# The first two up-projection tiles in token halves, ahead of the second half's norm

## The chip, the cores and the metric

The kernel runs on one core of a Trainium2 chip. The metric is the device time of one execution in microseconds, given as the median of several executions of the same program. The engines in what follows are PE (TensorE, matmuls), PEld (its weight loads), DVE (VectorE), ACT (ScalarE), POOL (GpSimd) and SP (the queue that issues DMAs).

## What is computed

One layer of a decoder trunk: attention and a state-space model side by side, an output projection, then a gated MLP. There are 256 tokens, 2048 model columns and 5632 columns in the MLP. The change is at the seam between the output projection and the MLP's up projection. Cut to what is computed there:

```python
mix = merged @ w_out                              # 256 x 2048
x = x + (1.0 + gt_m) * rmsnorm(mix, g_post_mix)
h = rmsnorm(x, g_pre_ffn) * (1.0 + sc_f) + sh_f   # 256 x 2048
up = causal_depthwise_conv(h @ w_up, conv_w, conv_b)   # 2048 -> 2 x 5632
val, gate = up[..., :D_FF], up[..., D_FF:]
ff = (gelu(gate) * val) @ w_down
x = x + (1.0 + gt_f) * rmsnorm(ff, g_post_ffn)
```

## The kernel before

The output projection accumulates `mix` in eight banks of PSUM, `acc[tt * 4 + n]`: two halves `tt` of 128 tokens by four quarters `n` of 512 columns. The last three of its 16 chunks are held back and then run bank by bank (`proj_held`, nine matmuls of 128x512 each), so that a bank is done while the next ones still run.

For each token half and quarter the seam then does: a square and sum of the bank on ACT (`sq`), a product with the gain on DVE (`gain`), and once all four sums of a half are there, its rstd (`rstd_start`, `rstd_end`; the last step, a power, runs on POOL). With it `x_add` makes the new x on DVE and `x_turn` transposes it on PE, four transposes of 128x128 to a quarter. `x_scale` takes them out of PSUM on DVE. `x_split` writes them as two numbers, a high part (a cast on ACT) and a low part (a subtraction on DVE or POOL, by its last argument: "ag" is ACT and POOL, "av" is ACT and DVE), into the four tiles `h2`, each of which holds four chunks of 128 model columns, and in each chunk the high parts of 256 tokens and then the low parts.

The up projection has 88 tiles, `up_mm(f, vg, parts)`, for 44 values of `f` and value or gate. Each reads 1 MB of weights, which `hl_up` loads and splits into high and low parts in two pieces (`h_wup`, `l_wup`, 128x1024 each, in a pool of five buffers of each kind). A tile is 16 chunks of two matmuls: the high weights against high and low tokens (512 columns) and the low weights against the high tokens (256 columns), both in a 32-bit type rounded for the matmul.

The scale by the second norm's rstd is put off: it is a factor of each token, made beside the first tiles (eight squares of x on ACT, two small matmuls with a diagonal, `ps_rn`), and `up_tile` applies it after the matmul. Between the tiles PE also computes the MLP's shift vector from weight granules (`ps_ada`, 32 matmuls to a pair of granules, and two column sums by `sel`).

What sets the order: PE's order follows the code through this seam, and so do DVE, ACT and POOL, since `in_order` adds a dependency from each of their instructions to the one before. Past the seam a scheduler places the instructions of all engines but SP, and so lets the shift matmuls slip between those of the tiles. SP issues its DMAs in the order of the code. The raw loads share six buffers of 1 MB (`raw`, and the two `prods`).

## Time and profile before

| | us |
|---|---|
| median of the three timed runs (1186.97 to 1190.68) | 1189.53 |
| the profiled execution | 1187.82 |
| its span in the profile | 1186.0 |
| PE busy in the span | 1128.9 |
| DVE busy | 874.6 |
| ACT busy | 547.2 |

The profile is of one execution, and its rows count from the start of the span. A row of the timeline gives the start, the time for which it lasts, the engine, the line, what is written and read, and what the engine waited for. Starts of one engine's rows may overlap: an instruction is in flight while the next begins, so the distance between starts says what one costs in a row of them. Plain f32 matmuls and transposes are recorded with their passes, so a plain f32 matmul has two records.

### The profile page before, as it was taken

The numbers are of one execution on the slowest core, as the hardware profiler recorded it, in microseconds if no ns is written. First come the engines' busy times: TensorE is split into PE (matmuls) and PEld (weight loads), VectorE is DVE, ScalarE is ACT, GpSimd is POOL, SyncE is SP. The second block draws the span as 40 slices with busy tenths as digits, with TensorE's granted clock in tenths as the row PEclk, the third lists the DMA queues.
The fourth block names the chain that finished last, engine by engine and source line by source line (L and its number), as shares of the span: only waits on it lengthen the run. The fifth ranks groups of instructions, "written<-read, shape, count | busy, mean of one in ns | idle before, by whom it ended". The sixth has DMA issues, their size and how long they took to land.

```text
span 1186.0 us, 18905 instructions
## 1 busy us (share of the span) xinstructions
PE 1128.9 (95%) x7542; PEld 945.5 (80%) x7542; DVE 874.6 (74%) x1386; ACT 547.2 (46%) x911; POOL 109.2 (9%) x107
## 2 busy tenths in 40 slices
PE   6999996988999799999999999999999999999996
PEld 4788875767787588888888888888888788888885
DVE  6687645775699778668999998986676766767555
ACT  3222131362534364446666556555555544444443
POOL 7404111004200320000000000000000000000002
PEclk8999999898999899999999999999999999999998
DMA  9899989388799668886787777775555787777712
GB/s 383 309 371 340 363 279 342 121 353 320 261 343 391 241 253 337 326 297 249 255 313 284 283 284 290 279 283 188 203 178 189 259 296 280 264 298 280 264 69 72
DMA packets 50234, 325.88 MB, mean 275 GB/s; under 512 B 6609, under 2 KB 8833, under 8 KB 13537
## 3 DMA queue, kind: packets, MB, share of 16 engines
q1 hardware_dynamic: 47152, 316.87, 71.7%
q0 software_dynamic: 2848, 7.75, 2.0%
q8 instruction: 59, 0.97, 0.3%
q14 instruction: 31, 0.25, 0.1%
q10 hardware_dynamic: 144, 0.05, 0.0%
HBM read 317.27 MB, written 7.37 MB: 274 GB/s over the span
## 4 chain that ended last, share of the span: by engine, by line
PE 77%; DVE 10%; issue 7%; DMA 3%; ACT 2%; POOL 1%; SPq 0%; DVEq 0%; ACTq 0%; POOLq 0%
PE ps_u L1235 28%; PE dn L562 15%; PE ps_u L1237 14%; PE accA L395 8%; PE ps_ada L155 3%; DVE l_wout L72 2%; PE ps_g L1033 2%; DVE ada L142 2%; PE accB L603 1%; DMA U<-ud 1%; PE mix L553 1%; DMA wglu<-in_w_glu_dram 1%; DVE scn L72 1%; DMA ud<-uT 1%; PE ps_y L809 1%
## 5 line engine op out<-in xcount | busy, mean ns | idle before, releaser
L543 ACT CAST h_wup<-wup 128x1024 fp32r<-128x1024 f32 x170 | 178.8, 1052 | 196.6 <-PE ps_u L1235 181.2
L544 DVE TENSOR_TENSOR l_wup<-wup,h_wup 128x1024 fp32r<-128x1024 f32 x170 | 207.9, 1223 | 83.3 <-ACT h_wup L543 79.8
L1235 PE MATMUL ps_u<-h2A,h_wup 128*128 128x512 f32 x704 | 251.5, 398 | 0.0
L1235 PE MATMUL ps_u<-h2B,h_wup 128*128 128x512 f32 x704 | 249.1, 394 | 0.0
L1237 PE MATMUL ps_u<-h2A,l_wup 128*128 128x256 f32 x704 | 196.4, 279 | 0.0
L1237 PE MATMUL ps_u<-h2B,l_wup 128*128 128x256 f32 x704 | 195.8, 278 | 0.0
L1235 PEld LDWEIGHTS ps_u<-h2A,h_wup 128*128 128x128 f32 x704 | 132.8, 189 | 31.3 <-issue 1.0
L1235 PEld LDWEIGHTS ps_u<-h2B,h_wup 128*128 128x128 f32 x704 | 132.0, 188 | 30.9 <-issue 0.4
L544 DVE TENSOR_TENSOR l_wdn<-wdn,h_wdn 128x1024 fp32r<-128x1024 f32 x88 | 107.6, 1224 | 65.7 <-ACT h_wdn L543 65.6
L1237 PEld LDWEIGHTS ps_u<-h2A,l_wup 128*128 128x128 f32 x704 | 133.2, 189 | 0.6 <-issue 0.4
L1237 PEld LDWEIGHTS ps_u<-h2B,l_wup 128*128 128x128 f32 x704 | 132.3, 188 | 0.4 <-issue 0.4
L543 ACT CAST h_wdn<-wdn 128x1024 fp32r<-128x1024 f32 x88 | 92.6, 1053 | 78.7 <-PE dn L562 70.4
L395 PE MATMUL accA<-hT,win 128*128 128x256 f32 x448 | 108.1, 387 | 0.0
L562 PE MATMUL dn<-h_wdn,fl 128*128 128x512 f32 x336 | 104.6, 396 | 1.4 <-DVE fl L544 1.4
L562 PE MATMUL dn<-l_wdn,fh 128*128 128x512 f32 x336 | 105.7, 395 | 0.0
L562 PE MATMUL dn<-h_wdn,fh 128*128 128x512 f32 x336 | 105.5, 396 | 0.0
L395 PEld LDWEIGHTS accA<-hT,win 128*128 128x128 f32 x448 | 82.0, 191 | 14.8 <-issue 5.1
L142 DVE CUSTOM_DVE_ANT_0 ada<-ada,cbc 128x2048 f32<-128x2048 f32 x38 | 87.8, 2319 | 0.2 <-DMA ada<-in_w_ada_dram 0.2
L562 PEld LDWEIGHTS dn<-h_wdn,fl 128*128 128x128 f32 x336 | 63.0, 188 | 17.0 <-DVE fl L544 1.9
L562 PEld LDWEIGHTS dn<-l_wdn,fh 128*128 128x128 f32 x336 | 63.1, 188 | 15.3
L562 PEld LDWEIGHTS dn<-h_wdn,fh 128*128 128x128 f32 x336 | 63.1, 188 | 15.2
L1377 DVE CUSTOM_DVE_ANT_0 wupt<-wupt,shbc 128x2048 f32<-128x2048 f32 x22 | 50.2, 2284 | 0.5 <-DMA wupt<-in_w_up_t_dram 0.5
(356 smaller groups left out, 1517.5 us busy)
## 6 DMA issues: line engine op xcount, KB each, us to landing
wup<-in_w_up_dram SPq DMA_DIRECT2D x88, 1024.0 KB, 5.0
ada<-in_w_ada_dram SPq DMA_DIRECT2D x64, 1024.0 KB, 6.8
wdn<-in_w_down_dram SPq DMA_DIRECT2D x44, 1024.0 KB, 4.9
wupt<-in_w_up_t_dram SPq DMA_DIRECT2D x22, 1024.0 KB, 6.3
scm<-in_w_ada_dram SPq DMA_DIRECT2D x16, 1024.0 KB, 9.0
shm<-in_w_ada_dram SPq DMA_DIRECT2D x16, 1024.0 KB, 6.1
wout<-in_w_out_dram SPq DMA_DIRECT2D x16, 1024.0 KB, 6.2
win<-in_w_in_a_dram SPq DMA_DIRECT2D x16, 896.0 KB, 7.4
```

The source lines that it names most:

```text
L72: self.last = self.no_earlier(getattr(self.e, name)(*args, **kw))
L142: return nc.vector.tensor_tensor_reduce(t, t, cbc, 1.0, 0.0, ALU.mult, ALU.add, accum_out=dst)
L155: PE.matmul(ps[32 * j:32 * j + 32, v * P:(v + 1) * P], lhsT=csil[:, kc:kc + 1].to_broadcast([P, 32]), rhs=t[:, kc * P:(kc + 1) * P], start ...
L395: PE.matmul(accA[ct // 2][:, (ct % 2) * S:(ct % 2 + 1) * S], lhsT=winA[k][:, ct * P:(ct + 1) * P], rhs=hk, start=(k == 0 and ct % 2 == 0), ...
L543: (A.copy if e[0] == "a" else V.tensor_copy)(hi, src)
L544: (V if e[1] == "v" else G).tensor_sub(lo, src, hi.bitcast(F32))
L553: PE.matmul(acc[tt * 4 + n], lhsT=a_[:, tk], rhs=b_[:, n2 * 512:(n2 + 1) * 512], start=False, stop=(kk == nk - 1 and last))
L562: PE.matmul(acc[tt * 4 + half * 2 + n2], lhsT=a_[:, tk], rhs=b_[:, n2 * 512:(n2 + 1) * 512], start=(kk == 0 and first), stop=(kk == nk - 1 ...
L1033: PE.matmul(psg[ct][:, :S], lhsT=wg_[ct // 2][:, (ct % 2 * 8 + k) * P:(ct % 2 * 8 + k + 1) * P], rhs=zf[:, k], start=(k == 0), stop=(k == 7))
L1235: PE.matmul(ps, lhsT=wh[:, ks], rhs=h2[kk // 4][:, kk % 4].rearrange("p a b -> p (a b)"), start=(kk == 0), stop=(kk == KD - 1), skip_group ...
L1237: PE.matmul(ps[:, :S], lhsT=wl[:, ks], rhs=h2_of(kk)[0], start=False, stop=(kk == KD - 1), skip_group_check=True)
L1377: V.tensor_tensor_reduce(t, t, shbc[0], 1.0, 0.0, ALU.mult, ALU.add, accum_out=rlate[:, vg, f:f + 1])
```

## The change

A new helper, `up_half(ps, parts, tt)`, does an up tile for one half of the tokens: 16 chunks of a matmul with 2 x 128 columns (high and low tokens of the half) and one with 128 columns. Tiles (0, 0) and (0, 1), which were two calls of `up_mm`, become four calls of it, each with 32 matmuls, and two of the four stand among the steps of the second half's norm. The weights of tile (0, 1) are loaded and split earlier in the code. The last two held banks of the second token half now stand behind the four `x_add` of the first half, and its last `x_split` has its low part on DVE instead of POOL. Tile (1, 0) is computed where (0, 1) was, and the weights of (1, 1) are asked for there.

```diff
+    def up_half(ps, parts, tt):
+
+        tk = slice(tt * P, (tt + 1) * P)
+        pv2 = ps.rearrange("p (a b) -> p a b", a=2)
+        for half in range(2):
+            wh, wl = parts[half]
+            for k in range(8):
+                kk, ks = half * 8 + k, slice(k * P, (k + 1) * P)
+                PE.matmul(pv2[:, :, tk], lhsT=wh[:, ks], rhs=h2[kk // 4][:, kk % 4, :, tk], start=(tt == 0 and kk == 0),
+                          stop=(kk == KD - 1), skip_group_check=True)
+                PE.matmul(ps[:, tk], lhsT=wl[:, ks], rhs=h2_of(kk)[0][:, tk], start=False, stop=(kk == KD - 1),
+                          skip_group_check=True)
...
-    for n in range(3):
-        proj_held(acc, held, 1, n)
+    proj_held(acc, held, 1, 0)
+    proj_held(acc, held, 1, 1)
     x_add(0, 0)
     sq(1, 0)
     gain(1, 0)
     x_add(0, 1)
     sq(1, 1)
     gain(1, 1)
-    proj_held(acc, held, 1, 3)
     x_scale(0, 0)
     x_split(0, 0, "ag")
     x_add(0, 2)
     x_scale(0, 1)
-    sq(1, 2)
     x_split(0, 1, "ag")
     x_add(0, 3)
+    proj_held(acc, held, 1, 2)
+    x_scale(0, 2)
+    x_split(0, 2, "ag")
+    sq(1, 2)
+    x_scale(0, 3)
+    x_split(0, 3, "av")
     rstd_start(24, nrm[:, 2, 1:2])
     gain(1, 2)
+    proj_held(acc, held, 1, 3)
+
+    ups.append(hl_up(0, 1, "ag"))
+    early = [bank(0, "ps_u")]
+    up_half(early[0], ups[0], 0)
     sq(1, 3)
-    x_scale(0, 2)
     rstd_end(24)
     gain(1, 3)
-    x_scale(0, 3)
-    x_split(0, 2, "ag")
-    x_split(0, 3, "ag")
     x_add(1, 0)
     x_add(1, 1)
+    early.append(bank(1, "ps_u"))
     x_scale(1, 0)
     x_split(1, 0, "ag")
     x_add(1, 2)
     x_scale(1, 1)
     x_split(1, 1, "ag")
+    up_half(early[1], ups[1], 0)
     x_add(1, 3)
     x_scale(1, 2)
     x_scale(1, 3)
     x_split(1, 2, "av")
     x_split(1, 3, "av")
-    early = [up_mm(0, 0, ups.pop(0))]
-    ups.extend((hl_up(0, 1, "ag"), hl_up(1, 0)))
+    up_half(early[0], ups.pop(0), 1)
+    up_half(early[1], ups.pop(0), 1)
+    ups.append(hl_up(1, 0))
...
-    early.append(up_mm(0, 1, ups.pop(0)))
+    ups.append(hl_up(1, 1))
+    early.append(up_mm(1, 0, ups.pop(0)))
...
-        if 2 < n_ < 2 * KF:
+        if 3 < n_ < 2 * KF:
             ups.append(hl_up(n_ // 2, n_ % 2))
-        ps = up_mm(f, vg, ups.pop(0)) if f else early[vg]
+        ps = early.pop(0) if early else up_mm(f, vg, ups.pop(0))
```

Three places in the order of the instructions follow. The names are the program's: `mix_2643` is the sixth held bank, `mix_2704` and `mix_2705` the seventh and the eighth, `ps_x` the transposes, `x_3184` and `x_3186` the x of the first and of the second token half, `prod_3204` and `prod_3205` their products, `stat` the sums and the rstd.

PE before, from the end of the eighth held bank to the first up tile:

```order
L553 MATMUL mix_2705<-l_wout,mh_2980 128x512
L553 MATMUL mix_2705<-h_wout,ml_2754 128x512
L1217 MATMUL ps_x_3316<-c_71,x_3184 128x128 x4
L1217 MATMUL ps_x_3327<-c_71,x_3184 128x128 x4
L1217 MATMUL ps_x_3347<-c_71,x_3186 128x128 x4
L1217 MATMUL ps_x_3353<-c_71,x_3186 128x128 x4
L1217 MATMUL ps_x_3362<-c_71,x_3186 128x128 x4
L1217 MATMUL ps_x_3371<-c_71,x_3186 128x128 x4
L1235 MATMUL ps_u<-h2A_3200,h_wup 128x512
```

PE now, from the end of the sixth held bank to the start of the seventh:

```order
L553 MATMUL mix_2643<-l_wout,mh_2980 128x512
L553 MATMUL mix_2643<-h_wout,ml_2754 128x512
L1217 MATMUL ps_x_3277<-c_71,x_3184 128x128 x4
L1217 MATMUL ps_x_3286<-c_71,x_3184 128x128 x4
L1217 MATMUL ps_x_3298<-c_71,x_3184 128x128 x4
L1217 MATMUL ps_x_3307<-c_71,x_3184 128x128 x4
L553 MATMUL mix_2704<-h_wout,mh_2935 128x512
```

PE now, from the end of tile (0, 0)'s first half to the start of tile (0, 1)'s first half:

```order
L1237 MATMUL ps_u<-h2B_3203,h_wup 128x2x128
L1239 MATMUL ps_u<-h2B_3203,l_wup 128x128
L1217 MATMUL ps_x_3390<-c_71,x_3186 128x128 x4
L1217 MATMUL ps_x_3396<-c_71,x_3186 128x128 x4
L1217 MATMUL ps_x_3406<-c_71,x_3186 128x128 x4
L1237 MATMUL ps_u<-h2A_3200,h_wup 128x2x128
L1239 MATMUL ps_u<-h2A_3200,l_wup 128x128
```

All 16 transposes of the first half now stand ahead of the seventh and the eighth bank, where two quarters stood ahead of the eighth and two behind it; and a half tile stands between the first half's transposes and the second's.

ACT before, from the first cast of a token quarter to the first weight cast:

```order
L72 CAST h2A_3200<-prod_3204 128x4x128
L72 ACTIVATE junk,stat<-mix_2704 128x512
L72 CAST h2A_3201<-prod_3204 128x4x128
L72 ACTIVATE junk,stat<-mix_2705 128x512
L72 CAST h2B_3202<-prod_3204 128x4x128
L72 CAST h2B_3203<-prod_3204 128x4x128
L72 CAST h2A_3200<-prod_3205 128x4x128
L72 CAST h2A_3201<-prod_3205 128x4x128
L72 CAST h2B_3202<-prod_3205 128x4x128
L72 CAST h2B_3203<-prod_3205 128x4x128
L72 CAST h_wup<-wup_3415 128x1024 x2
```

ACT now, in the same place:

```order
L72 CAST h2A_3200<-prod_3204 128x4x128
L72 CAST h2A_3201<-prod_3204 128x4x128
L72 CAST h2B_3202<-prod_3204 128x4x128
L72 ACTIVATE junk,stat<-mix_2704 128x512
L72 CAST h2B_3203<-prod_3204 128x4x128
L72 CAST h_wup<-wup_3341 128x1024 x2
L72 ACTIVATE junk,stat<-mix_2705 128x512
L72 CAST h2A_3200<-prod_3205 128x4x128
```

The weight casts of tile (0, 1) have moved from behind all token casts to a place ahead of the eighth bank's square.

POOL, the difference from before (-) to now (+), from the low parts of the first token half on:

```order
 L72 TENSOR_TENSOR h2A_3200<-prod_3204,h2A_3200 128x4x128
 L72 TENSOR_TENSOR h2A_3201<-prod_3204,h2A_3201 128x4x128
+L72 TENSOR_TENSOR h2B_3202<-prod_3204,h2B_3202 128x4x128
+L72 TENSOR_TENSOR l_wup<-wup_3341,h_wup 128x1024 x2
 L72 TENSOR_TENSOR stat<-stat,neg_half 128x1
-L72 TENSOR_TENSOR h2B_3202<-prod_3204,h2B_3202 128x4x128
-L72 TENSOR_TENSOR h2B_3203<-prod_3204,h2B_3203 128x4x128
 L72 TENSOR_TENSOR h2A_3200<-prod_3205,h2A_3200 128x4x128
 L72 TENSOR_TENSOR h2A_3201<-prod_3205,h2A_3201 128x4x128
-L72 TENSOR_TENSOR l_wup<-wup_3415,h_wup 128x1024 x2
 L72 TENSOR_TENSOR stat<-stat,neg_half 128x1 x2
```

The two low parts of tile (0, 1)'s weights now stand ahead of the power of the second half's rstd (the first `stat` row), where they stood behind all low parts of the tokens.

## Rows read from the trace of the kernel before

**Rows 1.** The waits of PE from 437 us on: total, times, longest.

```profile
PE dn L562 <- DVE fl L544: 1.4, 1, 1.4
```

**Rows 2.** Stretches: length, busy time (instructions) of each engine, granted clock, DMA.

```profile
405.00:410.00 5.00, 1.27 (x7) 1.03 (x8) 4.96 (x10) 1.45 (x4) 4.37 (x4) 0.85 0.00 0
410.00:415.00 5.00, 3.52 (x16) 2.32 (x14) 4.75 (x6) 1.45 (x3) 3.09 (x3) 0.50 0.59 210
415.00:420.00 5.00, 5.00 (x27) 4.13 (x26) 2.41 (x4) 4.20 (x6) 2.55 (x2) 0.62 0.31 72
408.50:409.00 0.50, 0.00 (x0) 0.00 (x0) 0.50 (x1) 0.26 (x1) 0.45 (x2) 0.53 0.00 0
418.50:419.00 0.50, 0.50 (x4) 0.40 (x3) 0.00 (x0) 0.50 (x2) 0.50 (x1) 0.73 0.94 115
```

**Rows 3.** Timeline of PE through the seam: start, length, line, out<-in, count.

```profile
397.28 0.39 PE L553 MATMUL mix<-h_wout,ml 128*128 128x512 f32 x1
...
405.34 0.66 PE L1217 MATMUL ps_x<-c,x 128*128 128x128 f32 x4 [0.60 <-DVE stat L72]
...
414.20 1.11 PE L1217 MATMUL ps_x<-c,x 128*128 128x128 f32 x4 [0.77 <-DVE x L72]
414.97 0.78 PE L1235 MATMUL ps_u<-h2A,h_wup 128*128 128x512 f32 x1
415.54 0.41 PE L1237 MATMUL ps_u<-h2A,l_wup 128*128 128x256 f32 x1
415.76 0.63 PE L1235 MATMUL ps_u<-h2A,h_wup 128*128 128x512 f32 x1
```

**Rows 4.** Timeline of DVE through the seam.

```profile
403.90 1.39 DVE L72 SCALAR_TENSOR_TENSOR x<-prod,stat,x 128x512 f32<-128x512 f32 x1
...
411.53 0.74 DVE L72 SCALAR_TENSOR_TENSOR x<-prod,stat,x 128x512 f32<-128x512 f32 x1
412.21 0.69 DVE L72 TENSOR_TENSOR prod<-ps_x,scale 128x512 f32<-128x512 f32 x1
...
415.96 1.46 DVE L72 TENSOR_TENSOR h2B<-prod,h2B 128x512 fp32r<-128x512 f32 x2
```

**Rows 5.** Timeline of ACT through the seam.

```profile
403.27 0.59 ACT L72 ACTIVATE junk<-mix 128x512 f32<-128x512 f32 x1
...
404.01 0.62 ACT L72 CAST h2A<-prod 128x512 fp32r<-128x512 f32 x1
...
416.61 4.10 ACT L72 CAST h_wup<-wup 128x1024 fp32r<-128x1024 f32 x4
```

**Rows 6.** Timeline of POOL: the power of the second half's rstd.

```profile
406.99 0.56 POOL L72 TENSOR_TENSOR stat<-stat,neg_half 128x1 f32<-128x1 f32 x1 [0.58 <-DVE stat L72]
```

**Rows 7.** The weights' low parts on POOL: count, ns min/median/max, first and last start.

```profile
L72 POOL TENSOR_TENSOR l_wup<-wup,h_wup x2: 2389/2889/3389, 417.7 to 420.1; 128x1024 fp32r<-128x1024 f32 x2
```

**Rows 8.** Timeline of PE at full clock, behind the seam.

```profile
435.26 0.27 PE L1237 MATMUL ps_u<-h2B,l_wup 128*128 128x256 f32 x1
435.37 0.40 PE L1235 MATMUL ps_u<-h2B,h_wup 128*128 128x512 f32 x1
435.60 0.28 PE L1237 MATMUL ps_u<-h2B,l_wup 128*128 128x256 f32 x1
...
437.45 0.40 PE L1235 MATMUL ps_u<-h2A,h_wup 128*128 128x512 f32 x1
...
442.97 1.95 PE L155 MATMUL ps_ada<-ada,csil 128*32 128x128 f32 x64
```

**Rows 9.** Timeline of the weight loads there.

```profile
434.46 0.53 PEld L162 LDWEIGHTS ps_ada<-sel,parts 128*128 128x128 f32 x4
...
435.26 0.19 PEld L1235 LDWEIGHTS ps_u<-h2B,h_wup 128*128 128x128 f32 x1
```

**Rows 10.** The page's group of plain f32 matmuls with 256 columns: count, busy us, mean ns.

```profile
L395 PE MATMUL accA<-hT,win 128*128 128x256 f32 x448 | 108.1, 387 | 0.0
```

## Prediction

> **What bounds the kernel now.** The page's table of engines has PE as the busiest, so the list of waits is read next, for PE, from 437 us to the end: one wait of 1.4 us [rows 1]. From the fourth up tile on (start 437.45, [rows 8]) PE is the bound, and whatever the fourth tile gains or loses goes into the time whole, as long as weights come in time. The stage that the change touches is the place left with holes. The table of stretches shows PE busy for 1.27 of the 5 us at 405 to 410, and the granted clock falling from 1.00 to 0.50, that is from 2.4 to 1.2 GHz, at 408.5 and coming back at about 418.7 [rows 2]. From 405.34 to 414.97 PE did nothing but transposes (the first and the last four in [rows 3]) and the clock, once down, stayed down; it rose 3.8 us after the dense up matmuls began at 414.97. From the end of the sixth of the eight held banks (397.28 + 0.23 = 397.51, [rows 3]) to the fourth tile's start are 39.9 us. The work in it at full clock is 18 held matmuls of 0.23, 32 transposes of 0.11, three tiles of 5.66 (16 pairs of 0.35, [rows 8]), one pair of shift granules 1.95 [rows 8], and 0.7 of small matmuls: 27.2 us. So 12.7 us are waits and low clock: that is all that the change can win.
>
> The change fills the hole with the first token half's matmuls, and pays for that by moving other work. Four things decide.
>
> **1. Two held banks move behind the transposes.** PE now does its four first-half transposes right behind the sixth bank, then the last two banks (18 matmuls). Up to there VectorE's order is the same, so the fourth row of additions still ends at 403.90 + 1.39 = 405.29 [rows 4], and the fourth transposes run at 405.34 as before [rows 3]. PE now has only transposes from 397.51 to about 406. In before, a stretch of transposes alone went to the low clock and stayed there, so I take it that this one does too, and that the clock comes back some 2 to 4 us into the dense matmuls. At half clock a held matmul takes 0.43, near twice the full rate: 7 in 3.0 us, then 11 of 0.23, 5.5 in all. Bank 6 is done at 409.7, bank 7 at 411.7.
>
> **2. The casts and low parts of the second tile's weights stand in the middle of the second half's norm.** ScalarE has the square of bank 6 once it is done, then the cast of the first half's last quarter, then the two weight casts, then the square of bank 7. From a square to the next start 0.74, a cast 0.62, a weight cast 4.10 / 4 = 1.03 [rows 5]: 409.7, 410.5, 411.1, first weight cast done 412.1; bank 7's square done at 413.9. GpSimd is worse: the two low parts (128x1024) stand ahead of the power that makes the second half's rstd. One took 2.39, the other 3.39 [rows 7]; the first began with VectorE idle, the second ran wholly beside VectorE's own low parts. VectorE has little to do then, so I take 2.39: 412.1 + 4.8 = 416.9, and the power (0.56) ends at 417.45. Before, it started at 406.99 [rows 6]. Without those two ahead of it the power could end at 414.6; so this order costs 2.9 us, and 4.9 at the slower duration. Behind the power in GpSimd's queue are two low parts of the second half, and behind its result are VectorE's four additions and then PE's transposes.
>
> **3. PE in the meantime.** The first half of tile 0 begins at 411.7 without a wait: its low parts are done at 408 on GpSimd, and by 412 on VectorE, where only the last four chunks need it. Its length turns on a form that the trace doesn't have: a matmul with 128 columns in this number type. By columns, 0.23 for 512 and 0.12 for 256 [rows 8], it would be 0.06. But each needs its own weights. A 512-column matmul starts at 435.37, 0.11 after its weight load at 435.26, and that load begins with the matmul before it; four one-column matmuls on 128x128 weights had their loads (0.53 - 0.19) / 3 = 0.11 apart [rows 8, 9]. The upper bound is the plain f32 matmul: 108.1 us for 224 of 256 columns (448 records, two each), so 0.24 for 128 [rows 10]. I take 0.11, the row of the same weight load. A half tile is then 16 x (0.12 + 0.11) = 3.7 us, against 2.83 by columns and 5.7 at the f32 rate.
> The Trainium skill ("TensorE: Matmul & The Clock Gate", section "Back-to-back issue gap") gives about 81 ns for a sustained matmul of 128 columns with its weight load. By that figure a half tile is 3.2 us and the sum below about 1.5 us less; no row here has that case, and the loads of 0.11 stand against it.
>
> So half 0 of tile 0 ends at 415.4, and PE waits: addition 417.5 to 418.25, transposes 1.11 at the low clock [rows 3] to 419.35, scaling 0.69 and the third addition 0.74 [rows 4] to 420.8, four transposes at (1.11 - 0.27) / 4 = 0.21 each to 421.7. Six microseconds with nothing dense: the clock is low again. Half 0 of tile 1 starts at 421.7; for 3.8 us a pair takes 0.22 + 0.22 [rows 3], 8.6 of 16, then 7.4 of 0.23: 427.2. The fourth transposes (0.44) end at 427.6.
>
> **4. From there it is dense.** Second half of tile 0: 3.7, and 17 of the 32 shift matmuls that now stand in it (1.0): 432.3. Second half of tile 1: 436.0. Tile 2, whole: 5.66, 441.65. The rest of the shift pair and the row-norm matmuls, 1.25: 442.9. The two column sums that stood before the fourth tile, and now in it, 0.34: 443.2 to compare with 437.45.
> What is hidden: VectorE's last two low parts of the second half (1.46 for two, [rows 4]) are ready at 429.7, about when the ninth chunk comes. The third tile's weights are cast from 429 and low by 432.6, needed at 436.0. ScalarE's eight squares then run to about 436.8 and the fourth tile's weights are low at 441.1, the diagonals that PE needs before the fourth tile at 441.7, needed at 442.3: 0.6 us of cover, and if it fails PE pays the excess. On the DMA queue the fourth tile's weights take the place of a shift granule, and that granule now waits for the first half's products (412); it is wanted at 430, 18 us later.
>
> **Sum.** 443.2 - 437.45 = +5.8 us. The profiled execution took 1187.82 (span 1186.0 and 1.8 around it), so 1193.6; it lies 1.7 below the median of the three timed runs. Against the median, 1189.53 + 5.8 = **1195.3 us**. Put otherwise: one fall of the clock becomes two, the thin stretch of 15 us becomes two of 8.5 and 6, and 0.8 us of weight loads are added to each half tile.
>
> **The rivals.**
> *Columns set the price (A).* A 128-column matmul at 0.06: the two dense halves save 0.8 each and the half at low clock 1.1, so -2.7, 1192.6. For it: the line through 512 and 256 columns. Against it: the load spacing in [rows 9].
> The Trainium skill (same page, section "Weight-path perf modes — Fast Weight Load (FWL) and DoubleRow") says that weights of 128 columns in a type other than FP32 are loaded faster of their own accord. Were that so for this type, A would hold; the loads of up weights and of plain f32 weights both last 0.19 here [rows 9], so the trace gives no sign of it.
> *Not slower: the clock stays full (B).* If the transposes, with what stands between, keep 2.4 GHz from 397 to 421, the held banks take 4.1 instead of 5.5 and start 0.4 earlier, bank 6 is done 1.8 earlier and with it the whole chain to the power; the transposes save 0.5 and half 0 of tile 1 saves 1.8: -4.1, 1191.2, no change that can be told. It decides from the clock reading 1.00 at 405 and at 420. Against it: transposes alone did not lift the clock in [rows 2, 3].
> *The f32 rate (C).* 128 columns at 0.24: two dense halves +2.0 each, the half at low clock +2.1, the first half hidden in the wait: +6.1, 1201.4.
> *The low parts at 3.39 each on GpSimd (D)*: +2.0, 1197.3, if VectorE's work meets them.
> *A gain* would need the second half's norm to come nearly as early as before. The chain of bank 6, casts, low parts and power has no such slack in any row: the norm comes 10 us later, and only one half tile (2.8 us by columns) stands ahead of its transposes to fill that, since the other stands behind them.
>
> **How the numbers follow.** Forecast with D, 1193.1 to 1198: 0.58. C: 0.12. A: 0.13. B: 0.12. A gain that no row prices: 0.05. About 0.3% (3.6 us) is what a measurement of this kernel can tell from no change, so slower starts at 1193.1. A sits 0.5 below that line and I put 0.05 of it above: slower 0.58 + 0.12 + 0.05 = 0.75, same 0.20, faster 0.05. The range reaches down to B (1191.0) and up to C (1201.5), leaving half of B, half of C and the gain outside, under 0.2.
>
> **What would show it.** In the changed profile: the power for the second half on GpSimd at about 417, behind two low parts; PE idle from about 415 to 418 and thin to 421.7; the clock at 0.50 around 402 to 408 and again around 419 to 425; a matmul starting 0.11 after one of 128 columns; the fourth tile's start near 443; and from there the same spacing as before, with no waits. The forecast is wrong if the power ends before 414, if the clock stays at 1.00, or if PE waits for weights after 443.

## The result and the profile after

| | before | after |
|---|---|---|
| median, us (16 runs each) | 1190.43 | 1197.55 |
| range of the runs, us | 1186.97 to 1197.55 | 1194.4 to 1208.43 |
| the profiled execution, us | 1187.82 | 1197.75 |
| PE busy in its span, us | 1128.9 | 1136.0 |

The changed kernel is slower: the ratio is 1.0061, with a 95% interval of 1.0041 to 1.0081. That is 7.3 us on the median of before (the two medians lie 7.1 apart), where +5.8 was forecast.

All starts in the profiled execution of after lie some 2 us later before the change begins: its first held matmul starts at 383.95, that of before at 381.89. Up to there the program is the same, so this is a difference between two executions. To compare the seams I count from that matmul. The fourth up tile starts 55.56 us after it in before (437.45 in [rows 8]) and 446.26 - 383.95 = 62.31 after it in after: 6.7 us later, and 7.9 later at the first matmul of the down projection.

The waits of PE for additions in after, from 380 to 445 us (total, times, longest):

```profile
PE ps_x L1217 <- DVE x L72: 8.3, 6, 2.8
```

From 445 us on there is one wait, the 1.4 us of [rows 1]. The waits for additions (`x`) ahead of the transposes were 5.9 us in before, and 0.6 more under the name `stat`.

The same stretches as in [rows 2] and two more (length, busy time and instructions of PE, PEld, DVE, ACT, POOL, granted clock, DMA share, GB/s):

```profile
400.00:405.00 5.00, 1.57 (x8) 0.93 (x8) 4.89 (x12) 1.53 (x7) 0.56 (x1) 0.91 0.65 238
405.00:410.00 5.00, 3.56 (x12) 2.87 (x13) 3.80 (x5) 1.85 (x3) 4.11 (x3) 0.50 0.01 5
410.00:415.00 5.00, 5.00 (x26) 4.26 (x26) 1.57 (x4) 3.06 (x6) 0.95 (x2) 0.91 0.11 15
415.00:420.00 5.00, 2.54 (x23) 2.40 (x21) 1.39 (x3) 0.62 (x3) 4.38 (x3) 1.00 0.63 215
420.00:425.00 5.00, 4.25 (x21) 3.62 (x22) 4.67 (x7) 1.44 (x3) 2.66 (x2) 0.61 0.48 193
425.00:430.00 5.00, 5.00 (x34) 5.00 (x34) 0.29 (x1) 0.41 (x1) 0.30 (x1) 0.70 0.00 0
```

A stretch of 5 us with a mean clock of 0.91 was 0.9 us at 0.50 and the rest at 1.00. Read so, the clock was low for about 6.8 us up to 410.9, came back, and was low again for about 6.9 us from 421.1 to 428. In before it was low once, for some 10 us [rows 2]. That is the forecast's "one fall becomes two".

PE through the seam (start, length, line, out<-in, count, the wait ahead of it); it answers to [rows 3] and [rows 8]:

```profile
383.95 0.39 PE L553 MATMUL mix<-h_wout,mh 128*128 128x512 f32 x1
...
407.56 1.11 PE L1217 MATMUL ps_x<-c,x 128*128 128x128 f32 x4 [0.77 <-DVE x L72]
408.33 0.78 PE L553 MATMUL mix<-h_wout,mh 128*128 128x512 f32 x1
...
413.74 0.28 PE L1237 MATMUL ps_u<-h2A,h_wup 128*128 128x256 f32 x1
413.85 0.22 PE L1239 MATMUL ps_u<-h2A,l_wup 128*128 128x128 f32 x1
413.91 0.34 PE L1237 MATMUL ps_u<-h2A,h_wup 128*128 128x256 f32 x1
414.08 0.22 PE L1239 MATMUL ps_u<-h2A,l_wup 128*128 128x128 f32 x1
...
417.32 0.22 PE L1239 MATMUL ps_u<-h2B,l_wup 128*128 128x128 f32 x1
420.22 1.58 PE L1217 MATMUL ps_x<-c,x 128*128 128x128 f32 x8 [2.68 <-DVE x L72]
422.33 1.11 PE L1217 MATMUL ps_x<-c,x 128*128 128x128 f32 x4 [0.53 <-DVE x L72]
423.09 0.56 PE L1237 MATMUL ps_u<-h2A,h_wup 128*128 128x256 f32 x1
...
429.06 0.62 PE L1217 MATMUL ps_x<-c,x 128*128 128x128 f32 x4
429.43 0.36 PE L1237 MATMUL ps_u<-h2A,h_wup 128*128 128x256 f32 x1
...
431.41 1.06 PE L155 MATMUL ps_ada<-ada,csil 128*32 128x128 f32 x26
...
433.46 0.42 PE L155 MATMUL ps_ada<-ada,csil 128*32 128x128 f32 x8
...
434.79 0.33 PE L1237 MATMUL ps_u<-h2A,h_wup 128*128 128x256 f32 x1
...
438.49 0.45 PE L1248 MATMUL ps_u<-h2A,h_wup 128*128 128x512 f32 x1
...
444.28 0.85 PE L155 MATMUL ps_ada<-ada,csil 128*32 128x128 f32 x20
...
445.70 0.62 PE L155 MATMUL ps_ada<-ada,csil 128*32 128x128 f32 x10
...
446.26 0.50 PE L1248 MATMUL ps_u<-h2A,h_wup 128*128 128x512 f32 x1
```

The reader is to see four things. The two held banks run behind the four transposes (408.33 to 413.74). The first half of tile (0,0) follows at once and costs 0.23 for a pair of matmuls (413.85 to 414.08 between the two of 128 columns). Then comes nothing but twelve transposes until 423.09. And from 429.06 PE is dense.

ACT, POOL and DVE between the seventh bank and the second half's additions; the power answers to [rows 6], the two low parts ahead of it to [rows 7]:

```profile
413.03 2.00 ACT L72 CAST h_wup<-wup 128x1024 fp32r<-128x1024 f32 x2
414.16 4.71 POOL L72 TENSOR_TENSOR l_wup<-wup,h_wup 128x1024 fp32r<-128x1024 f32 x2 [4.05 <-ACT h_wup L72]
418.83 0.56 POOL L72 TENSOR_TENSOR stat<-stat,neg_half 128x1 f32<-128x1 f32 x1
419.42 1.41 DVE L72 SCALAR_TENSOR_TENSOR x<-prod,stat,x 128x512 f32<-128x512 f32 x2 [2.96 <-POOL stat L72]
```

The power waits behind the two low parts on POOL, the additions wait 2.96 us for the power, and PE waits 2.68 us for the additions.

### The profile page after: what moved, and what is told of

Its sections match the earlier page's. It is cut to its first block, busy times and chain, and to the rows that moved or that the text cites. A ratio compares the mean times of both kernels' runs of the same rounds, so it can differ in the third digit from the quotient of the medians.

```text
span 1196.0 us, 19037 instructions
## 1 busy us (share of the span) xinstructions
PE 1136.0 (95%) x7606; PEld 954.1 (80%) x7606; DVE 871.2 (73%) x1387; ACT 546.3 (46%) x911; POOL 106.6 (9%) x106
## 4 chain that ended last, share of the span: by engine, by line
PE 61%; issue 22%; DVE 8%; DMA 4%; POOL 2%; ACT 2%; SPq 0%; DVEq 0%; POOLq 0%; ACTq 0%
PE ps_u L1248 27%; PE ps_u L1250 13%; PE accA L395 8%; PE ps_ada L155 3%; PE ps_g L1033 2%; DVE l_wout L72 2%; DVE ada L142 2%; PE accB L603 1%; DMA U<-ud 1%; PE ps_u L1237 1%; DMA wup<-in_w_up_dram 1%; DVE scn L72 1%; DMA wglu<-in_w_glu_dram 1%; PE ps_y L809 1%; DMA x<-in_x_dram 1%
## 5 line engine op out<-in xcount | busy, mean ns | idle before, releaser
L544 DVE TENSOR_TENSOR l_wup<-wup,h_wup 128x1024 fp32r<-128x1024 f32 x168 | 205.2, 1223 | 84.6 <-ACT h_wup L543 79.3
L1248 PE MATMUL ps_u<-h2B,h_wup 128*128 128x512 f32 x688 | 243.7, 395 | 0.0
L1248 PE MATMUL ps_u<-h2A,h_wup 128*128 128x512 f32 x688 | 243.6, 395 | 0.0
L1250 PE MATMUL ps_u<-h2A,l_wup 128*128 128x256 f32 x688 | 191.8, 279 | 0.0
L1250 PE MATMUL ps_u<-h2B,l_wup 128*128 128x256 f32 x688 | 191.6, 278 | 0.0
L1248 PEld LDWEIGHTS ps_u<-h2B,h_wup 128*128 128x128 f32 x688 | 129.0, 188 | 30.2 <-issue 0.4
L1248 PEld LDWEIGHTS ps_u<-h2A,h_wup 128*128 128x128 f32 x688 | 128.9, 188 | 30.0 <-issue 0.4
L1250 PEld LDWEIGHTS ps_u<-h2A,l_wup 128*128 128x128 f32 x688 | 129.4, 188 | 0.8 <-issue 0.6
L1250 PEld LDWEIGHTS ps_u<-h2B,l_wup 128*128 128x128 f32 x688 | 129.4, 188 | 0.4 <-issue 0.4
```

Of the source, the lines that this page charges most:

```text
L544: (V if e[1] == "v" else G).tensor_sub(lo, src, hi.bitcast(F32))
L1248: PE.matmul(ps, lhsT=wh[:, ks], rhs=h2[kk // 4][:, kk % 4].rearrange("p a b -> p (a b)"), start=(kk == 0), stop=(kk == KD - 1), skip_group ...
L1250: PE.matmul(ps[:, :S], lhsT=wl[:, ks], rhs=h2_of(kk)[0], start=False, stop=(kk == KD - 1), skip_group_check=True)
```

## The experiments

Theory 1 is the prediction's: the second half's norm is late behind the low parts (part 2), the banks behind the transposes delay it too (part 1), and each half tile pays for its own weight loads (part 3). Theory 2 puts all down to the half tiles, theory 3 to the banks and the clock alone. Times of the table are medians of their own runs, ratios against runs of before on the same chip; a ratio need not be the quotient of two medians.

A single execution also has a difference ahead of the change, in code that all these kernels share. ScalarE's squares of the first half stand behind its casts of the first up tile's weights, and those wait for a transfer. In before the last matmul of the first bank starts at 387.06, but the square of that bank starts only at 395.07, behind the casts, and the first half's power at 398.92:

```profile
393.17 2.00 ACT L72 CAST h_wup<-wup 128x1024 fp32r<-128x1024 f32 x2 [7.15 <-DMA wup<-in_w_up_dram]
...
398.92 0.55 POOL L72 TENSOR_TENSOR stat<-stat,neg_half 128x1 f32<-128x1 f32 x1 [80.55 <-DVE stat L72]
```

The casts start 11.28 us after the first held matmul in before, 9.23 in "halves in place" and 9.91 in "low parts on VectorE", and the first half's power 17.03, 14.98 and 15.66 after it (17.22 in after). So the table counts the fourth tile's start twice: "from held" from the first held matmul, less the 55.56 us of before, and "from power" from the first half's power, less the 38.53 of before. Only the second leaves out what happened ahead of the change. "Norm" is the time from the first half's power to the second half's, 8.1 us in before. "First down matmul" is counted from the first held matmul. "Low" is the time at 0.50 in the seam, worked out from stretches of a quarter of a microsecond. In the profiled executions of four kernels (marked *) the later up tiles take up to some 0.1 us more each, far behind the seam and with at most 0.3 us of waits of PE in all; for those the column of the first down matmul is left empty. What the casts ahead of the first half's squares cost, no run tried.

| kernel | median, us | ratio (95%) | norm, us | fourth tile from held, us | fourth tile from power, us | first down matmul, us | low, us |
|---|---|---|---|---|---|---|---|
| after | 1197.55 | 1.0061 (1.0041 to 1.0081) | 17.7 | +6.7 | +6.6 | +7.9 | 13.7 |
| after, weights behind the power | 1196.39 | 1.0070 (1.0046 to 1.0095) | 14.0 | +6.5 | +6.5 | +7.7 | 13.7 |
| after, banks first | 1193.46 | 1.0034 (1.0020 to 1.0047) | 14.4 | +3.1 | +3.9 | +4.7 | 10.2 |
| before, halves in place | 1193.45 | 1.0031 (1.0013 to 1.0049) | 8.3 | +0.9 | +3.0 | +1.5 | 6.8 |
| before, weights early | 1194.83 | 1.0048 (1.0029 to 1.0067) | 12.1 | +4.1 | +4.1 | +4.5 | 13.7 |
| after, low parts on VectorE | 1194.21 | 1.0026 (1.0001 to 1.0051) | 16.7 | +1.6 | +3.0 | +3.1 | 6.8 |
| before, first half in pieces | 1186.84 | 0.9965 (0.9934 to 0.9996) | 8.1 | -4.0 | -3.5 | -4.0 | 0 |
| the same again* | 1187.24 | 0.9991 (0.9964 to 1.0018) | 8.1 | -2.4 | -2.4 |  | 3.4 |
| before, idle matmuls | 1188.14 | 0.9984 (0.9961 to 1.0006) | 8.1 | -2.6 | -1.6 | -2.1 | 0 |
| after, idle matmuls* | 1193.97 | 1.0029 (1.0005 to 1.0054) | 17.6 | +4.1 | +3.9 |  | 6.8 |
| after, banks first and VectorE* | 1193.16 | 1.0022 (0.9993 to 1.0051) | 12.9 | +2.5 | +2.7 |  | 10.2 |
| before, third tile early | 1190.29 | 0.9997 (0.9971 to 1.0023) | 8.1 | -0.9 | -0.3 | +0.5 | 10.2 |
| first half in pieces, idle matmuls* | 1186.17 | 0.9970 (0.9950 to 0.9990) | 8.1 | -2.5 | -2.1 |  | 0 |

### The weights of tile (0,1) behind the power

```
-    ups.append(hl_up(0, 1, "ag"))
     early = [bank(0, "ps_u")]
     up_half(early[0], ups[0], 0)
     sq(1, 3)
     rstd_end(24)
+    ups.append(hl_up(0, 1, "ag"))
     gain(1, 3)
```

> The changed kernel, with the loading, casts and low parts of tile (0, 1)'s weights moved behind the power of the second token half's norm; nothing else. Theory 1 (the prediction's: the power waits behind the two low parts on GpSimd, 2.9 us, and behind the weight casts on ScalarE): the power ends some 3 to 4 us earlier than in the changed kernel, PE's wait behind tile (0, 0)'s first half shrinks by as much, the fourth tile starts 3 to 4 us earlier; time +3.5 us against before (changed kernel: +7). Theory 2 (the loss is the price of computing in halves, the weight loads of short matmuls): the queue's order is worth nothing, still +7. Theory 3 (the two banks behind the transposes and the fall of the clock make the loss): +6 to +7, since both stay.

This one fell out against theory 1. The power did end earlier: it starts at 414.54, which is 30.93 after the first held matmul, and 34.88 in after, so 3.95 us sooner (3.7 from the first half's power). The fourth tile gained 0.2 of it, from the power nothing, and the median nothing that can be told. POOL and DVE of this kernel:

```profile
414.54 0.56 POOL L72 TENSOR_TENSOR stat<-stat,neg_half 128x1 f32<-128x1 f32 x1 [5.00 <-DVE stat L72]
415.23 5.64 POOL L72 TENSOR_TENSOR l_wup<-wup,h_wup 128x1024 fp32r<-128x1024 f32 x2
...
415.13 0.75 DVE L72 SCALAR_TENSOR_TENSOR x<-prod,stat,x 128x512 f32<-128x512 f32 x1
415.80 2.86 DVE L72 SCALAR_TENSOR_TENSOR x<-prod,stat,x 128x512 f32<-128x512 f32 x1
...
419.18 2.23 DVE L72 SCALAR_TENSOR_TENSOR x<-prod,stat,x 128x512 f32<-128x512 f32 x1
```

The two low parts now run beside the very additions that the power releases. The first two additions take 0.75 and 2.86, together 3.53 us, and 1.41 in after; the third takes 2.23, and 0.74 in after with POOL idle. The first began 0.1 us ahead of a subtraction. The other two end 0.5 us after one does (418.11 and 420.87), so they wait for it rather than run slowly. So 2.1 + 1.5 = 3.6 of the 3.95 us go back on VectorE. The scaling on VectorE, which reads PSUM, takes 0.68 in both.
The Trainium skill ("SBUF — State Buffer", section "Who interferes with whom") says that a VectorE instruction with two inputs in SBUF contends with a GpSimd instruction that reads SBUF. The trace agrees: 0.74 without such a neighbour, 2.86 and 2.23 for the two additions that began while a subtraction ran. Before has it too: its first two additions of the second half take 2.98 us (from 408.02) beside low parts of tokens on GpSimd (from 407.52). No run moved those.

### The banks ahead of the third transposes again

```
     proj_held(acc, held, 1, 1)
+    proj_held(acc, held, 1, 2)
     x_add(0, 0)
...
     gain(1, 1)
+    proj_held(acc, held, 1, 3)
     x_scale(0, 0)
...
     x_add(0, 3)
-    proj_held(acc, held, 1, 2)
     x_scale(0, 2)
...
     gain(1, 2)
-    proj_held(acc, held, 1, 3)
```

> The changed kernel, with the seventh and eighth held banks put back where before had them on PE (the seventh ahead of the first transposes, the eighth behind two quarters of them); nothing else. Theory 1: bank 6's square and with it casts, low parts and power come some 3 us earlier; the fourth tile starts 3 to 4 us earlier, +3.5 us against before. Theory 2 (price of halves): +7, unchanged. Theory 3 (banks and clock make the whole loss): back to before, 0 to +1.

As theory 1 has it: the fourth tile comes 3.7 us sooner than in after (2.7 from the first half's power) and the median falls by 4.1. The clock keeps 1.00 through the first half's transposes and falls once, not twice.

### Halves in place

```
-    early = [up_mm(0, 0, ups.pop(0))]
+    early = [bank(0, "ps_u"), bank(1, "ps_u")]
+    up_half(early[0], ups[0], 0)
+    up_half(early[0], ups.pop(0), 1)
...
-    early.append(up_mm(0, 1, ups.pop(0)))
+    up_half(early[1], ups[0], 0)
+    up_half(early[1], ups.pop(0), 1)
```

> The kernel before, with tiles (0, 0) and (0, 1) each computed as two token halves where their whole tiles stood; no other step moves. It measures the price of halves alone. Theory 1: a pair of a 256-column and a 128-column matmul takes 0.23 us instead of 0.177, four halves of 16 pairs: +3.4 us for the fourth tile's start, +3.5 in time. Theory 2 (halves are the loss): +7, which would need a pair of 0.29. If columns alone set the price: 0.

The median of 11 runs is 3.2 us above that of before (1190.21), which is four times the 0.8 of the prediction. Its profiled execution shows only +0.9 from the first held matmul, because its first half's power came 2.05 us sooner than in before; from that power it is +3.0. In that execution the clock was low for 6.8 us instead of 10. The price of halves is thus measured; that the weight loads make it, and no other cost of each matmul, is read from their spacing and not shown by a run.

### The weights early in the kernel before

```
     gain(1, 2)
+    ups.append(hl_up(0, 1, "ag"))
...
-    ups.extend((hl_up(0, 1, "ag"), hl_up(1, 0)))
+    ups.append(hl_up(1, 0))
```

> The kernel before, with the loading, casts and low parts of tile (0, 1)'s weights moved ahead of the square of the last bank and so of the second half's power, as the change has it; whole tiles, banks and transposes as before. It takes the queue's cost alone. Theory 1: the power ends 4 us later than in before (about 411.5 instead of 407.5), tile (0, 0) starts that much later, +4 to +5 us. Theories 2 and 3: no change, 0 to +1.

Part 2 by itself, with no half tile anywhere: +4.1 us at the fourth tile. POOL and PE of this kernel:

```profile
408.59 4.66 POOL L72 TENSOR_TENSOR l_wup<-wup,h_wup 128x1024 fp32r<-128x1024 f32 x2
413.20 0.56 POOL L72 TENSOR_TENSOR stat<-stat,neg_half 128x1 f32<-128x1 f32 x1
...
415.59 1.12 PE L1217 MATMUL ps_x<-c,x 128*128 128x128 f32 x4 [7.38 <-DVE x L72]
```

PE's wait for the second half is 7.4 us where it was 3.4 in before, and the clock is low for 3.4 us longer. The line of before:

```profile
409.39 1.11 PE L1217 MATMUL ps_x<-c,x 128*128 128x128 f32 x4 [3.39 <-DVE x L72]
```

### The low parts on VectorE

```
-    ups.append(hl_up(0, 1, "ag"))
+    ups.append(hl_up(0, 1, "av"))
```

> The changed kernel with one word changed: the two low parts of tile (0,1)'s weights are made by VectorE instead of GpSimd, so that nothing stands ahead of the second half's power on GpSimd and GpSimd is idle while VectorE adds. Theory 1 (the prediction's: the two low parts cost the norm time, by queue or, as the run with the weights behind the power suggests, by slowing VectorE's additions from the neighbouring engine): VectorE waits for banks there anyway, so the two low parts (about 1.2 us each) cost it little; the power ends about 3.5 us earlier than in the changed kernel, the additions take 0.74 each, the second half's transposes come right behind half 0 of tile 0, and the fourth up tile starts 2.0 to 3.0 us earlier: 1194.5 to 1195.5. Theory 2 (only the halves' own weight loads cost): no change against the changed kernel, 1197.5 within 1. If the low parts on VectorE themselves delay the gain and the additions: 1196.5.

One letter takes 5.1 us off the fourth tile as counted from the first held matmul. But 1.6 of that lies ahead of the change, in the first half's power; from there it is 3.6, still more than was expected. DVE, POOL, ACT and PE first, then stretches of PE alone (length, busy, clock, DMA):

```profile
417.77 2.35 DVE L72 TENSOR_TENSOR l_wup<-wup,h_wup 128x1024 fp32r<-128x1024 f32 x2
420.04 0.21 DVE L72 TENSOR_SCALAR stat<-stat 128x1 f32<-128x1 f32 x1
...
420.92 1.42 DVE L72 SCALAR_TENSOR_TENSOR x<-prod,stat,x 128x512 f32<-128x512 f32 x2
...
420.33 0.56 POOL L72 TENSOR_TENSOR stat<-stat,neg_half 128x1 f32<-128x1 f32 x1 [7.74 <-DVE stat L72]
...
418.51 0.20 ACT L72 ACTIVATION_READ_ACCUMULATOR junk<-mix 128x1 f32 x1
...
421.73 1.32 PE L1217 MATMUL ps_x<-c,x 128*128 128x128 f32 x8 [1.07 <-DVE x L72]
```

```profile
420.00:425.00 5.00, 3.15 (x25) 1.00 0.83 311
425.00:430.00 5.00, 5.00 (x47) 1.00 0.01 3
```

The low parts are not free on VectorE: the eighth bank's sum is there at 418.71, and the step on VectorE that the power waits for starts at 420.04, behind them, so they cost 1.3 us. On GpSimd in after they cost 2.9: the same step is done at 415.86 (415.65 and 0.21), and the power starts at 418.83. Counted from the first half's power, the second half's starts only 1.0 us sooner than in after, where 3.5 was expected, as the eighth bank also ends 0.6 later there, counted the same way. The additions keep their 0.71 each. PE's wait ahead of the second half's transposes is 1.07 us instead of 2.68, and now the clock stays at 1.00: the half of tile (0,1) runs at the full rate, which gives the other 2.6 us of the 3.6. The two rows of stretches stand against 0.61 and 0.70 in after.

### The first half of tile (0,0) in pieces, nothing else moved

```
     x_split(0, 3, "ag")
+    early = [bank(0, "ps_u")]
+    up_part(early[0], ups[0], 0, range(8))
     x_add(1, 0)
     x_add(1, 1)
+    up_part(early[0], ups[0], 0, range(8, 12))
...
     x_add(1, 2)
+    up_part(early[0], ups[0], 0, range(12, 16))
...
-    early = [up_mm(0, 0, ups.pop(0))]
+    up_part(early[0], ups.pop(0), 1, range(16))
```

`up_part` is `up_half` for a given range of the 16 chunks.

> The kernel before with only one thing of the change: the first half of tokens of tile (0,0) is computed early, in three pieces set where TensorE waits (eight contraction chunks behind the first half's last transposes, four behind the second half's second transposes, four behind its third), its second half in the old place, tile (0,1) whole; held banks, weight casts and low parts and third tile as before. Theory 1: the price is 0.8 us for each half tile (1.7 in all), and some 3.7 us of work go into waits that the norm leaves anyway, with the clock perhaps up: the fourth tile starts 1.0 to 2.5 us earlier than in the kernel before: 1188 to 1189.5. Theory 2 (the price of halves is not hidden): +1.5 to +2, 1192. Theory 3 (clock alone): as far as the granted clock stays at 1.00 from 405 to 419 us it gains 2 us more, and stays the same otherwise.

This is the idea of the change without its price: the norm's order is that of before, one tile instead of two pays for halves, and the first half stands in three waits that PE has anyway. Its fourth tile starts at 433.67, which is 51.60 after its first held matmul and 4.0 sooner than before (3.5 from the first half's power), more than the 1.0 to 2.5 expected. Stretches of PE in this execution, and behind the next expectation those of a second set of runs of the same kernel:

```profile
405.00:410.00 5.00, 3.11 (x24) 1.00 0.00 0
410.00:415.00 5.00, 3.88 (x33) 1.00 0.61 213
```

> The kernel before with the first token half of tile (0,0) set in pieces into TensorE's waits, once more, since its interval reached up to 0.9996. Its trace has the fourth up tile 4.0 us earlier than the kernel before, with the granted clock at 1.00 throughout: ratio 0.9966 within 0.0015, below one. If the gain was the luck of one sitting: 1.000.

```profile
405.00:410.00 5.00, 3.89 (x29) 1.00 0.00 0
410.00:415.00 5.00, 2.89 (x19) 0.88 0.32 103
415.00:420.00 5.00, 5.00 (x55) 0.78 0.27 110
```

In [rows 2] PE was busy for 1.27 of the 5 us from 405 on, here for 3.1 to 3.9. In the second execution the clock fell all the same, for 3.4 us, and 1.6 of the 4.0 us were lost; 0.5 of these were lost already at the first half's power, so 1.1 go with the clock. The medians lie 4.1 and 2.4 us below those of before; the second interval reaches over 1, so the expected 0.9966 was missed there.

### Idle matmuls: the clock by itself

`spin(n, count)` issues matmuls of 512 columns on the first up weights, into a bank that the next tile overwrites. Nobody reads their results. In the kernel before:

```
     x_add(0, 3)
+    spin(0, 13)
...
     x_add(1, 0)
+    spin(0, 2)
     x_add(1, 1)
+    spin(0, 2)
...
     x_add(1, 2)
+    spin(0, 2)
```

> The kernel before with 19 matmuls of 512 columns added whose results nobody reads (thirteen behind the first half's last transposes, two behind each of the second half's first three), in a bank that the first up tile overwrites: TensorE is kept busy in the waits and nothing else is moved. It measures what the clock costs there. If the clock stays at 1.00 from 405 to 419 us: the first 3.8 us of dense up matmuls run at 0.23 for 512 columns instead of 0.42, which gives 1.9 us, and the transposes 0.3 to 0.5: 1188 us. If the clock falls all the same: 1190.2 within 0.5. If the added matmuls get in the way of the transposes: up to +1.5.

The clock stayed at 1.00 through the seam and the fourth tile came 2.6 us sooner (1.6 from the first half's power), the first down matmul 2.1. The median is 2.8 below before, though the interval reaches over 1. In the changed kernel:

```
     up_half(early[0], ups[0], 0)
+    spin(1, 11)
...
     x_add(1, 1)
+    spin(1, 2)
```

> The changed kernel with 13 matmuls of 512 columns added whose results nobody reads (eleven behind half 0 of tile (0,0), two behind the second half's second transposes). It measures the second fall of the clock by itself. If that fall is worth what the prediction took (half 0 of tile (0,1) at the low clock): that half takes 3.7 us instead of 5.9 and the transposes are at full clock, the fourth up tile starts 2.0 to 2.5 us earlier, 1195.2. If the clock falls in spite of the work: 1197.5 within 0.5. If something else than the clock sets that half: 1197.5 with the clock at 1.00.

Here the stretch in which after was at 0.61:

```profile
420.00:425.00 5.00, 4.68 (x40) 1.00 0.36 151
```

The fourth tile came 2.7 us sooner than in after: that is what the second fall costs.

### Banks first and low parts on VectorE

The edits of "the banks ahead of the third transposes again" and of "the low parts on VectorE" in one kernel; the latter's edit is:

```
-    ups.append(hl_up(0, 1, "ag"))
+    ups.append(hl_up(0, 1, "av"))
```

> The changed kernel with both parts of its order undone that cost time in the runs before: the two held banks ahead of the third transposes, as in the kernel before, and the low parts of tile (0,1)'s weights on VectorE instead of GpSimd; the four half tiles and the early third tile stay. Theory 1: what is left is the weight loads of four half tiles (4 x 0.8 = 3.2 us) and the shift work broken into more pieces (1.0), against 7.4 us of half tiles that now may stand in the waits; the fourth up tile at +1.0 to +2.5 us against the kernel before, since the two runs saved 3.6 and 5.1 us of the 6.7 and part of that is the same wait: 1191 to 1193. Rival (the savings add up whole): -2 us, 1188.5. Rival (the halves are the fault whatever the order): +3.5, 1194.

At +2.5 us (+2.7 from the first half's power) it is at the upper end of theory 1's span or just past it, and it can't be told from the low parts on VectorE alone (1.0022 and 1.0026). The banks come sooner, so the half tile does too, and it no longer stands where the wait is: PE waits 3.2 us, and the clock is low under the second half's transposes and the next half tile, as with the banks first alone:

```profile
415.00:420.00 5.00, 4.00 (x18) 0.50 0.53 203
420.00:425.00 5.00, 5.00 (x27) 0.55 0.00 0
```

The savings of the two edits are thus not a sum: from the first half's power they are 2.7 and 3.6 us alone and 3.9 together. Nor is the order wholly undone here. The norm still takes 12.9 us and not 8.1: ScalarE's casts of tile (0,1)'s weights (from 409.72) stand ahead of the eighth bank's square (411.61), and the step before the power waits from 412.30 to 413.73 for the low parts on VectorE. Four half tiles with the norm as in before, two of them in the waits, were not run.

### The third tile early, alone

```
     early.append(up_mm(0, 1, ups.pop(0)))
+    ups.append(hl_up(1, 1))
+    early.append(up_mm(1, 0, ups.pop(0)))
...
-        if 2 < n_ < 2 * KF:
+        if 3 < n_ < 2 * KF:
...
-        ps = up_mm(f, vg, ups.pop(0)) if f else early[vg]
+        ps = early.pop(0) if early else up_mm(f, vg, ups.pop(0))
```

> The kernel before with the last part of the change alone: the third up tile's matmuls and the fourth tile's weight casts move ahead of the diagonals and the row-norm matmuls. Theory 1: TensorE has no wait there in the kernel before that this could fill, and the same work stands in another order: the fourth up tile within 0.5 us, 1190.5. Rival (the eight squares and the diagonals come too late behind the fourth tile's casts): +1 to +2, 1192. Rival (it takes away a wait): -0.7.

No difference that can be told (0.9971 to 1.0023). By itself this part of the change neither gains nor costs anything beyond that.

### Both: pieces and idle matmuls

Against the kernel with the first half in pieces:

```
     up_part(early[0], ups[0], 0, range(8))
+    spin(1, 5)
     x_add(1, 0)
+    spin(1, 3)
     x_add(1, 1)
```

> The kernel with the first token half of tile (0,0) set in pieces into TensorE's waits, with eight matmuls of 512 columns added whose results nobody reads: five where TensorE waits 1.6 us for the second half's first transposes, three where it waits 1.0 us for the second. In one trace of that kernel the granted clock stayed at 1.00 and the fourth up tile came 4.0 us earlier than in the kernel before; in the other it fell to 0.50 for 4 us and the tile came 2.4 us earlier. Theory (the clock is all that differs between those two): with the waits filled the clock stays at 1.00, the fourth tile comes 4.0 us earlier, ratio 0.9966. Rival (the added matmuls delay the transposes, or the clock falls all the same): -2.4 or less, 0.998 or above.

```profile
405.00:410.00 5.00, 4.59 (x31) 1.00 0.00 0
```

The clock stayed up and the interval (0.9950 to 0.9990) lies below 1. The fourth tile reads -2.5, but in this execution a pair of shift granules (1.95 in [rows 8]) stands ahead of it and not behind; two tiles later, with the same shift work done, the kernel is 4.4 us ahead of before (64.80 against 69.27 after the first held matmul). Its median is the lowest here, 4.4 us under that of before: half a tile in the right place, and eight matmuls that compute nothing. Whether those eight add to the 4.1 and 2.4 us of the pieces alone can't be told.

## Why the prediction came out right

The forecast was 1195.3 us and slower; it came out 1197.55 and slower. 1.3 of the missing 2.25 us are in the difference itself (7.1 on the medians, 5.8 forecast), 0.9 are the median of before (1190.43 over 16 runs, 1189.53 over three). For the comparison of single times 2.1 us are taken off the times of after.

**Part 1, right.** The fourth transposes start at 407.56 - 2.1 = 405.5 (forecast 405.34). Clock low from about 404.1 - 2.1 = 402. The two banks take 408.33 to 413.74, 5.4 us (5.5). That they cost time by their place was shown: with them back the median is 4.1 us lower, and the fourth tile 2.7 sooner from the first half's power.

**Part 2, the time right, its reason half right.** The power ends at 419.39 - 2.1 = 417.3 (417.45), the low parts take 2.35 each (2.39, so rival D fell). The step "so this order costs 2.9 us" has its size right: the power could have started at 415.9 and started at 418.83. But it is incomplete. Taking the queue away gave nothing, because the same two low parts then hold up the additions on VectorE. The low parts on GpSimd cost their time there either ahead of the power or beside the additions; on VectorE they still cost 1.3. [rows 4] already held the sign of it, an addition of 1.39 beside one of 0.74, and the prediction read the two as durations to choose from and not as a sign of the neighbour.

**Part 3, right.** A half tile takes 3.7 us (3.7): 16 pairs of 0.23, from 413.74 to 417.32 and the last matmul behind it, so columns (A) and the f32 rate (C) both fell. The detail was wrong: a 128-column matmul starts 0.17 after the 256-column one ahead of it and the next starts 0.06 after that, not 0.11 each; only the pair is 0.23. The second half tile starts at 421.0 (421.7), since the clock fell later than assumed (at about 421.1 in after) and the first four transposes and part of the next four ran at the full rate, and takes 423.09 to 429.06, 5.97 us (5.5), since it also rose later. It ends at 427.0 (427.2): two misses of 0.7 and 0.5 us that cancel by luck. The clock fell under the transposes twice, so B fell; the price of the second fall, 2.7 us by the idle matmuls, is the 1.8 and 0.5 that B names for it within 0.4.
The Trainium skill's 81 ns for a 128-column matmul ("TensorE: Matmul & The Clock Gate", section "Back-to-back issue gap"), by which the sum would have been 1.5 us less, doesn't hold for this mix: sixteen pairs took 3.70 us.

**Part 4, the term that was mis-sized.** Second half of tile (0,0): 429.43 to 434.79, 5.36 us, and not 4.7, since 17 of the 32 shift matmuls (34 records) in two pieces took 1.66 us and not 1.0. The second half of tile (0,1) is 3.70 as forecast. From the third tile's start (438.49) to the fourth's are 7.77 us, of which 5.66 are the tile and 2.11 the other 15 shift matmuls and the row norm, where 1.25 were forecast. The 32 shift matmuls last 1.06 + 0.42 + 0.85 + 0.62 = 2.95 us in four pieces; in one piece they were 1.95 [rows 8]. I had taken the price of one piece for work that the scheduler cuts into four. The trace of before had it already: behind its transposes a pair of granules runs in three pieces of 0.62, 0.42 and 1.51, 2.55 us together. So 0.7 + 0.9 = 1.5 us too little, 0.2 of it made up ahead. Behind the fourth tile another 1.1 us are lost up to the first down matmul, of which 0.34 were forecast (the two column sums); where the rest goes was not settled. The covers held: PE waits for nothing behind the seam but the old 1.4 us.

**The gain.** The prediction gave it 0.05, as "a gain that no row prices". That holds for the change as it is. But the hole in [rows 2] could be filled: half a tile in pieces, with the norm left alone, is worth 2.4 to 4.1 us in the medians of two sets of runs, of which the smaller can't be told from nothing. What made the change slower is in part what was moved past the second half's norm (two banks, two casts and two low parts) and in part the price of four half tiles, 3.2 us where they fill no wait; the first part was undone in steps, never whole.

## What to carry to other kernels

Work that is to fill a wait should not stand, on any engine, ahead of or beside the chain that ends the wait; here two subtractions on GpSimd held the power back by 2.9 us, or the additions by 3.6, and still the power by 1.3 once VectorE made them. A wait of PE with little in it costs twice, by itself and by the clock of the dense work behind it (2.7 us for the second fall in after), and two edits that shorten it need not add up. Before single executions are compared, look how far they differ ahead of the change: here by up to 2.2 us. Before a tile is cut, count its weight loads: two half tiles were 7.4 us where the whole was 5.66, so only the part that fits into the wait should be cut.

## What was not expected of the hardware

- Matmuls that compute nothing brought later work forward: 13 in the waits of after took away the second fall of the granted clock and brought the fourth tile 2.7 us sooner; 19 in the waits of before kept the clock at 1.00 and brought it 1.6 to 2.6 sooner, with a ratio whose interval reaches over 1.
- The same kernel kept the clock at 1.00 in one execution and had it at 0.50 for 3.4 us in another, with the same work in the seam and 1.1 us between them from the first half's power on. A forecast of the clock for a stretch that is filled by half holds for some executions only.
- An addition on VectorE (128x512, both inputs in SBUF) took 0.74 us alone and 2.86 and 2.23 when it began while a 128x1024 subtraction ran on GpSimd; it ended some 0.5 us after that subtraction, which itself only went from 2.35 to 2.8.
